# Gate and up of four expert ranks with the weights stationary and the tokens moving, with other slot counts

## The chip, the cores and the metric

One core of a Trainium2 chip runs the kernel; the other cores are idle. The metric is device time in microseconds (us) of one execution, as the median of several; lower is better. The engines are TensorE (PE; its weight loads are listed apart as PEld), VectorE (DVE), ScalarE (ACT), GpSimd (POOL) and SyncE (SP), beside 16 DMA engines.

## The reference

Two layers over 512 latent tokens (and 256 context tokens in the first one), width 1024. Layer 0 is a pooling and attention mixer and a dense SwiGLU, layer 1 latent attention and a mixture of eight experts, of which each token takes two. The change is in the experts:

```python
def moe_swiglu(h, router_w, w_gate, w_up, w_down):
    probs = jax.nn.softmax((tok @ router_w).astype(F32), axis=-1)
    top_p, top_e = lax.top_k(probs, TOP_K)
    top_p = top_p / jnp.sum(top_p, axis=-1, keepdims=True)
    ...
    hg = lax.ragged_dot(xs, w_gate, group_sizes)
    hu = lax.ragged_dot(xs, w_up, group_sizes)
    ys = lax.ragged_dot(jax.nn.silu(hg) * hu, w_down, group_sizes)
```

Each expert has gate and up of 1024 x 2816 and down of 2816 x 1024, all in float32. 512 tokens with two experts each make 1024 rows over the eight experts.

## The kernel before

**Split products.** Every float32 operand is split in two fp32r parts: hi is a rounded copy (`nc.scalar.copy`, ScalarE) and lo the rest (VectorE), both by `split` (L133). `mm3` (L108 to L110) makes a product of three matmuls: hi by hi, hi by lo, lo by hi. The first operand of a matmul is stationary (loaded into the array, a PEld record), the second one moves through it, a column at a time.

**Ranks and slots.** The experts are sorted by their number of tokens on the chip, and rank r gets a fixed count of slots, `CAPS[r]` (L32). A rank's slots are cut in tiles of up to 128 tokens (`rank_tiles`): 256 slots are two tiles, 192 one of 128 and one of 64. Tokens beyond a rank's slots would go to overflow tiles, run by a loop at the end (up to `NOVF` of them, each reading one expert's weights again); the loop runs as often as the routing finds such tiles. Results are written to the DRAM tensor `y_d`, from which each token gathers its two rows. Rows that no expert writes in time are zeroed first (L1220, at the start of `out_and_route`, six writes of 128 x 1024 on the POOL queue).

**One expert** (`expert`, L1503) works in 11 blocks of 256 hidden columns. For a block, `unit` (L1467) loads three pieces of 1 MB of weights (u_raw) and splits each into u_hi and u_lo: two for gate and up, one for down.

- `gate_up(b)`: for each tile of tokens, the tokens x (8 groups of 128 rows of the model width) are stationary, and the weights move: 512 columns, 256 of gate and 256 of up. The sum stands in one PSUM bank (tile name pz, two banks). A tile of 64 tokens (`half`) has its hi and lo side by side as one stationary of 128 columns (L1489, with one more matmul of 64, L1490), two matmuls in place of three; `fold` (L1494) then adds the two halves of the sum. ACT makes silu of the gate half (L1522), DVE the product with the up half (L1523), into sg, tokens by hidden columns.
- `turn(b)`: PE transposes sg in two pieces (L1531) into a bank named ptr or prb, and `split` makes hs of it, hidden columns by tokens.
- `down(b)`: hs is stationary, the down weights move, 512 columns at a time; sums stay in PSUM (pS), or are added up in SBUF (yacc) for the ranks of the second track while the first one runs.

The program gives gate and up of block b+1 ahead of down of block b, and turn of b+1 after it. Two tracks run interleaved: ranks 2, 0, 1 on one, ranks 3, 5, 6, 7, 4 on the other. `flow` (L55) lays their steps on one line: rank 2 beside the end of 3 and beside 5, rank 0 beside 6, rank 1 beside 7, rank 4 last with the rest of the line to itself. The framework that builds the program sets the final order on each engine and all waits.

**Token tiles.** `turn_tile` (L1439) transposes gathered tokens on PE and writes x, hi and lo, with the norm's gain and shift; `RUN_UP` says how many steps ahead of an expert each tile is gathered and turned.

**Names.** x: tokens; u_raw, u_hi, u_lo: weights; sg: gated hidden values; hs: their split transposes; pz, ptr, prb, pS: PSUM banks. L292, L408, L818 and L973 are lines of layers 0 and 1 ahead of the experts.

Of the kernel before, what the change touches and what calls it, by code (L numbers as in the profile page):

```python
# [18 lines left out]
D = 1024  # L19
KT = 8  # L20
# [10 lines left out]

CAPS = (256, 256, 192, 128, 128, 128, 64, 64)  # L32
NSLOT = sum(CAPS)
NOVF = 5
TRACKS = ((2, 0, 1), (3, 5, 6, 7, 4))
# [27 lines left out]
class Kernel:  # L63
# [484 lines left out]
    def layer0_mixer(self):  # L548
        nc, I, tc = self.nc, self.I, self.tc
        self.mix_d = self.dram.tile([KT - 2, 128, TA], F32, name="mix_d")  # L550
        with ExitStack() as ctx:
# [31 lines left out]
            blat = scaled(0, LAT)  # L583
            self.cos = self.const.tile([128, TL], F32, name="cos")
            self.sin = self.const.tile([128, TL], F32, name="sin")
            self.rot = self.const.tile([128, 128], F32, name="rot")
            self.pw = wk.tile([128, 2, 128], F32, name="poolw")
# [428 lines left out]
    def layer1_mixer(self, ctx):  # L1016
# [179 lines left out]
    def out_and_route(self, ctx):  # L1196
# [9 lines left out]
        nc.gpsimd.dma_start(rw, I["router"])  # L1206
        rc = wk.tile([128, 80], F32, name="rc")
        nc.gpsimd.dma_start(rc, I["rconst"])
        iota8, c7, lt = rc[:, 0:8], rc[:, 8:16], rc[:, 16:80].rearrange("p (a b) -> p a b", b=8)
        cb = wk.tile([128, 256], BF16, name="cb")  # L1210
        cf = wk.tile([128, 256], F32, name="cf")
# [127 lines left out]

        nc.vector.tensor_scalar(cap, rank, 5.5, None, op0=OP.is_lt)  # L1340
        nc.vector.scalar_tensor_tensor(cap, rank, 2.5, cap, op0=OP.is_lt, op1=OP.add)
        nc.vector.scalar_tensor_tensor(cap, rank, 1.5, cap, op0=OP.is_lt, op1=OP.add)
        nc.vector.tensor_scalar(cap, cap, 64.0, 64.0, op0=OP.mult, op1=OP.add)
        nc.vector.scalar_tensor_tensor(base, rank, 6.0, rank, op0=OP.min, op1=OP.add)
        nc.vector.scalar_tensor_tensor(base, rank, 3.0, base, op0=OP.min, op1=OP.add)
        nc.vector.scalar_tensor_tensor(base, rank, 2.0, base, op0=OP.min, op1=OP.add)
        nc.vector.tensor_scalar(base, base, 64.0, None, op0=OP.mult)
        nc.vector.tensor_sub(o, n, cap)
# [89 lines left out]

    def turn_tile(self, xg):  # L1439

        n = xg.shape[0]
        X = self.parts(self.xq, "x", 8, KT, n)
# [7 lines left out]
    def parts(self, pool, tag, bufs, k, n):  # L1450

        x = [pool.tile([128, k, 128], F32R, name=tag, bufs=bufs) for _ in range(n // 64)]
        return x if n == 128 else [x[0][:, :, :64], x[0][:, :, 64:], x[0]]

# [39 lines left out]
    def fold(self, ps):  # L1494

        nc = self.nc
        n = ps.shape[1]
        lo = self.xp.tile([64, 512], F32, name="fold", bufs=1)[:, :n]
        nc.scalar.copy(lo, ps[64:])
        nc.vector.tensor_add(lo, ps[:64], lo)  # L1500
        return lo

    def expert(self, reg, X, store, acc=None):  # L1503

        nc, xp = self.nc, self.xp
        NB = F // 256
        T = len(X)
        half = [len(x) == 3 for x in X]
        Y = acc or [self.ps.tile([128, D], F32, name="pS", bufs=2) for i in range(T)]
        H = {}  # L1510

        def gate_up(b):
            U = [self.unit(reg, 3 * b + i) for i in range(2)]
            U = [[v.rearrange("p (k f) -> p k f", f=512) for v in u] for u in U]
            for i in range(T):
# [4 lines left out]
                n = p.shape[0]  # L1520
                sg = xp.tile([128, 256], F32, name="sg", bufs=4)[:n]
                nc.scalar.activation(sg, p[:, :256], AF.Silu)  # L1522
                self.gated = nc.vector.tensor_mul(sg, sg, p[:, 256:])  # L1523
                H[b, i] = sg

        def turn(b):
            for i in range(T):
                n = H[b, i].shape[0]
                pt = self.tr_tile()[:, :2, :n]
                for k in range(2):  # L1530
                    nc.tensor.transpose(pt[:, k, :], H[b, i][:, k * 128:k * 128 + 128], self.ident[:n, :n])  # L1531
                h = self.parts(xp, "hs", 9, 2, n)
                self.split(h[0], h[1], pt)
                H[b, i] = h

        def down(b):
            dh, dl = self.unit(reg, 3 * b + 2)
            for i in range(T):
                h = H.pop((b, i))
                for s in range(2):  # L1540
                    o = s * 512
                    w = lambda k: (dh[:, k * D + o:k * D + o + 512], dl[:, k * D + o:k * D + o + 512])
                    y = Y[i][:, o:o + 512]
# [3 lines left out]
                    p = self.tr_tile().rearrange("p a b -> p (a b)")  # L1547
                    self.mm_tile(p, h, w, 2)
# [4 lines left out]

        gate_up(0)
        yield
        turn(0)
        for b in range(NB):
            if b + 1 < NB:
                gate_up(b + 1)
            down(b)  # L1560
            if b + 1 < NB:
                turn(b + 1)
                yield
        for i in range(T):
            n = 64 if half[i] else 128
            y = (acc[i] if acc else xp.tile([128, D], F32, name="xg", bufs=3))[:n]
            for s in (slice(0, 512), slice(512, 1024)):
                nc.vector.tensor_mul(y[:, s], self.fold(Y[i][:, s]) if half[i] else Y[i][:, s],
                                     self.g2row[:n, s])
            store(i, y)  # L1570
# [24 lines left out]

    def gather_y(self, acc, j, pool, place, tag, bufs):
# [4 lines left out]
        ys = [place.tile([128, D], F32, name=tag, bufs=bufs) for _ in range(2)]  # L1601
        for c, y in enumerate(ys):
# [14 lines left out]
    def moe(self, ctx):  # L1617
# [3 lines left out]
        with ExitStack() as c:  # L1621
            self.moe_pools(c, 2)
            xp = self.xp
            X, G, Sw, todo = {}, {}, [], {}
            order = flow()
# [10 lines left out]

            def turn(t, first):
                if first:
                    G[t] = self.turn_tile(G[t])
                X[t] = next(G[t], X.get(t))  # L1640
# [12 lines left out]
            def weigh():  # L1653

                with behind(tc, self.gathered):
                    nc.gpsimd.dma_start(fg, self.I["final_g"].to_broadcast([128, D]))
                sw = self.xq.tile([128, 2, 512], F32R, name="x", bufs=8)
                Sw.extend((sw[:, 0, :], sw[:, 1, :]))
                OH = self.onehot(last[0], self.i128)
# [13 lines left out]
            def sums(j):  # L1673

                with behind(tc, self.gated):
                    if j > 1:
                        next(G[j - 2], None)
                    if j < 4:
                        G[j] = self.gather_y(A[j], j, xp, *((self.xq, "x", 8) if j % 2 else (xp, "xg", 3)))
                        next(G[j])  # L1680
# [15 lines left out]
            def merge(y):  # L1696

                yh, yl = (self.xq.tile([128, D], F32R, name="x", bufs=8) for _ in range(2))
                for s in (slice(0, 512), slice(512, 1024)):
# [8 lines left out]

            x = X[rank_tiles(FIRST)[0]] = self.parts(self.xq, "x", 8, KT, 128)
            self.x_ins = [self.affine_half(x, 4 * i, pt, (nc.scalar, nc.vector)[i]) for i, pt in enumerate(self.first)]  # L1710
            E = {}
            for p, (r, step) in enumerate(order):
                if step == 0:
# [7 lines left out]
                    acc = [xp.tile([128, D], F32, name="yacc", bufs=1)] if p < at(TRACKS[0][-1], STEPS - 1) and r in TRACKS[1] else None  # L1721
                    E[r] = self.expert(reg, [X[t] for t in rank_tiles(r)], store, acc)
                next(E[r], None)
# [32 lines left out]
    def run(self):  # L1756
        with ExitStack() as ctx:
# [4 lines left out]
            with ExitStack() as c:  # L1762
                self.nraw, self.nhl = 3, 4
                self.wp = self.pool(c, "wp")
                self.big = self.pool(c, "big")
# [72 lines left out]
def layouts(inp):  # L1838
# [38 lines left out]
    e = np.arange(8, dtype=np.float32)  # L1877
    rc = np.concatenate([e, 7 - e, (e[None, :] < e[:, None]).astype(np.float32).reshape(-1)])
    A["rconst"] = np.ascontiguousarray(np.broadcast_to(rc, (128, 80)))
    p = np.arange(128, dtype=np.float32)  # L1880
# [39 lines left out]
```

## Time and profile before

| what | us |
|---|---|
| median of 3 runs (2325.4 to 2331.2) | 2327.38 |
| the profiled execution | 2319.6 |
| its span, first to last instruction | 2317.9 |
| PE busy in the span | 2251.2 |
| VectorE busy | 1765.4 |
| ScalarE busy | 1212.2 |
| GpSimd busy | 198.3 |

The granted clock of TensorE was 0.989 of full speed as a mean of the span. The experts take the time from about 1308 us to the end. In the rows further down, times are microseconds from the start of the span. Records of matmuls and of weight loads are longer than the distance between two of them, because they are pipelined: their pace is the distance between starts. A shape such as 128\*128 128x512 is the stationary (rows by columns) and then the output (rows by moving columns). "x8" is a count of like instructions merged in one line, and "<-DVE u_lo" behind an idle time names what ended it.

### The profile page before, as it was taken

The page shows a single profiled execution, that of the slowest core. Times are in us where ns is not written, and L with a number is a line of the kernel's source. Part 1 is how long each engine was busy: PE and PEld are TensorE (multiplying, and loading weights), DVE is VectorE, ACT ScalarE, POOL GpSimd, SP SyncE. Part 2 cuts the span into 40 slices and gives each one's busy share as a digit, 9 for nine tenths or more (in the row PEclk, how much of TensorE's full clock was granted, in tenths as well). Part 3 has the DMA queues.
Part 4 walks back from the last instruction along what each step waited for, and adds up shares of the span by engine and source line. Part 5 has one row for each costly group of instructions (what it writes and reads, how often), then busy time and mean ns, then how long its engine had stood idle before and what let it go on. Part 6 is the DMA issues. An engine that isn't in the chain of part 4 may idle for free.

```text
span 2317.9 us, 31085 instructions
## 1 busy us (share of the span) xinstructions
PE 2251.2 (97%) x11672; PEld 1833.2 (79%) x11672; DVE 1765.4 (76%) x2547; ACT 1212.2 (52%) x1690; POOL 198.3 (9%) x273
## 2 busy tenths in 40 slices
PE   8999998999999999999999899999999999999996
PEld 3777777899999988888888777777777777777774
DVE  4779876687877876477775798787877778777897
ACT  3445553453334432245553676566655666555764
POOL 0033410000000111000000000010000000000030
PEclk9999998999999999999999999999999999999998
DMA  7233322335444596311122797787777877777794
GB/s 295 80 105 106 107 77 95 110 132 165 143 141 152 198 377 240 126 42 42 35 85 78 275 362 293 282 304 274 266 276 275 315 263 288 267 285 272 275 399 175
DMA packets 97505, 467.97 MB, mean 202 GB/s; under 512 B 11232, under 2 KB 13664, under 8 KB 63556
## 3 DMA queue, kind: packets, MB, share of 16 engines
q1 hardware_dynamic: 76000, 386.83, 45.9%
q0 software_dynamic: 19680, 76.90, 9.2%
q10 hardware_dynamic: 1668, 2.18, 0.3%
q8 instruction: 94, 1.54, 0.3%
q14 instruction: 63, 0.52, 0.1%
HBM read 435.19 MB, written 30.68 MB: 201 GB/s over the span
## 4 chain that ended last, share of the span: by engine, by line
PE 85%; DVE 6%; ACT 2%; DMA 1%; issue 1%; POOL 0%; DVEq 0%; ACTq 0%
PE pz L109 11%; PE pz L108 11%; PE pz L110 11%; PE pS L818 10%; PE pS L973 5%; PE pz L818 4%; PE pS L108 4%; PE pS L109 4%; PE pS L110 3%; PE pz L1490 3%; PE pz L1489 3%; PE pz L973 2%; PE prb L108 1%; PE prb L109 1%; PE prb L110 1%; DVE u_lo L133 1%
## 5 line engine op out<-in xcount | busy, mean ns | idle before, releaser
L133 DVE TENSOR_TENSOR u_lo<-u_raw,u_hi 128x2048 fp32r<-128x2048 f32 x264 | 601.8, 2285 | 154.7 <-ACT u_hi L133 154.5
L133 ACT CAST u_hi<-u_raw 128x2048 fp32r<-128x2048 f32 x264 | 502.4, 1909 | 199.5 <-issue 69.6
L109 PE MATMUL pz<-u_lo,x 128*128 128x512 f32 x704 | 283.7, 403 | 6.2 <-DVE u_lo L133 6.0
L108 PE MATMUL pz<-u_hi,x 128*128 128x512 f32 x704 | 282.0, 401 | 0.5 <-ACT u_hi L133 0.5
L110 PE MATMUL pz<-u_hi,x 128*128 128x512 f32 x704 | 279.9, 398 | 0.0
L108 PE MATMUL pz<-ah,w_hi 128*128 128x512 f32 (+1 forms) x513 | 183.4, 358 | 1.1 <-DVE n_tmp L325 0.6
L109 PE MATMUL pz<-al,w_hi 128*128 128x512 f32 (+1 forms) x513 | 178.8, 349 | 0.0
L110 PE MATMUL pz<-ah,w_lo 128*128 128x512 f32 (+1 forms) x513 | 178.2, 348 | 0.0
L109 PEld LDWEIGHTS pz<-u_lo,x 128*128 128x128 f32 x704 | 132.5, 188 | 46.0 <-DVE u_lo L133 18.7
L108 PEld LDWEIGHTS pz<-u_hi,x 128*128 128x128 f32 x704 | 132.4, 188 | 29.9 <-ACT u_hi L133 1.0
L110 PEld LDWEIGHTS pz<-u_hi,x 128*128 128x128 f32 x704 | 132.5, 188 | 28.5
L292 DVE SCALAR_TENSOR_TENSOR n_acc<-ms 128x1024 bf16<-128x1024 f32 x80 | 97.4, 1217 | 19.0 <-DMA ms<-in_mod_t_dram 18.9
L108 PEld LDWEIGHTS pz<-ah,w_hi 128*128 128x128 f32 x513 | 97.3, 190 | 14.9 <-issue 0.9
L97 ACT CAST w_hi<-w_raw 128x1024 fp32r<-128x1024 f32 (+2 forms) x69 | 58.6, 851 | 93.3 <-PE pz L109 63.2
L110 PEld LDWEIGHTS pz<-ah,w_lo 128*128 128x128 f32 x513 | 97.2, 190 | 11.0 <-issue 0.5
L109 PEld LDWEIGHTS pz<-al,w_hi 128*128 128x128 f32 x513 | 97.6, 190 | 10.5 <-issue 0.7
L109 PE MATMUL pS<-u_lo,hs 128*128 128x512 f32 x264 | 105.1, 398 | 0.7 <-DVE u_lo L133 0.7
L1489 PE MATMUL pz<-u_hi,x 128*128 128x512 f32 x264 | 105.3, 399 | 0.0
L108 PE MATMUL pS<-u_hi,hs 128*128 128x512 f32 x264 | 104.6, 396 | 0.5 <-ACT hs L133 0.5
L110 PE MATMUL pS<-u_hi,hs 128*128 128x512 f32 x264 | 104.6, 396 | 0.0
L1490 PE MATMUL pz<-u_lo,x 128*64 128x512 f32 x264 | 98.5, 394 | 0.0
L408 ACT ACTIVATE P<-pS,mx 128x768 f32<-128x768 f32 (+1 forms) x104 | 83.3, 804 | 19.7 <-DVE mx L407 19.4
(561 smaller groups left out, 5431.8 us busy)
## 6 DMA issues: line engine op xcount, KB each, us to landing
u_raw<-in_moe_w_dram SPq DMA_DIRECT2D x264, 1024.0 KB, 4.9
ms<-in_mod_t_dram POOLq DMA_DIRECT2D x56, 512.0 KB, 4.9
hr<-hid_d SPq DMA_DIRECT2D x38, 384.0 KB, 6.0
w_raw<-in_w_gate_dram SPq DMA_DIRECT2D x28, 512.0 KB, 3.5
w_raw<-in_w_in_dram SPq DMA_DIRECT2D x27, 512.0 KB, 3.3
u<-in_w_up_dram SPq DMA_DIRECT2D x22, 512.0 KB, 3.7
w_raw<-in_w_dn_dram SPq DMA_DIRECT2D x22, 512.0 KB, 4.7
hid_d<-hm POOLq DMA_DIRECT2D x22, 384.0 KB, 3.1
```

What stands on the lines that cost most here:

```text
L97: nc.scalar.copy(hi[:, :n], raw[:, :n])
L108: nc.tensor.matmul(ps, wh, xh, start=first and i == 0, stop=False)
L109: nc.tensor.matmul(ps, wh, xl, start=False, stop=False)
L110: ins = nc.tensor.matmul(ps, wl, xh, start=False, stop=last and i == n - 1)
L133: return nc.scalar.copy(hi, src), nc.vector.tensor_sub(lo, src, hi)
L292: nc.vector.scalar_tensor_tensor(self.m_junk, w, 1.0, self.crow[:, cd, :], op0=OP.mult, op1=OP.mult, accum_out=self.mods[:, layer, cd, n:n ...
L408: self.exped = nc.scalar.activation(P, S, AF.Exp, bias=nm, accum_out=z)
L818: nc.tensor.matmul(ps, w[m][:, c], x[n][:, k, :], start=first and k == i == 0, stop=k == 3 and i == 2, skip_group_check=True)
L973: nc.tensor.matmul((pl, px)[cd][d], W[w][:, d * 128:d * 128 + 128], x[v][:, s], start=n == i == 0 and not (cd and d % 2), stop=n == NF - 1 ...
L1489: m = [lambda s, e: self.nc.tensor.matmul(ps, x[2][:, k, :], w(k)[0], start=s, stop=e), lambda s, e: self.nc.tensor.matmul(ps[:64], x[0][: ...
L1490: lambda s, e: self.nc.tensor.matmul(ps[:64], x[0][:, k, :], w(k)[1], start=s, stop=e)]
```

## The change

The slots become 216, 216, 192, 128, 128, 72, 64, 64 (1080 in all, before 1216), with up to seven overflow tiles in place of five. For ranks 0, 1, 2 (`APART`) and 5 (`JOINED`) gate and up are done the other way round: pieces of 128 weight columns are stationary and all tokens of the rank (216, 216, 192 or 72) move through them. For rank 5, hi and lo of the tokens lie side by side, so that one matmul of 144 columns makes two of the three products. Gate and up then stand in two banks, hidden columns by tokens, and need no transposing; sg is split as it is. The other ranks are as before. The token tiles get other shapes and buffer counts: per rank one pair of tiles (xa) for the ranks of `APART`, four buffers of x for the rest. `cos`, `sin` and `rot` move to a pool of their own that is closed before the experts, which frees their room. The zeros are written at the start of layer 1's attention, as 32 writes of 128 x 256 in place of six of 128 x 1024. The routing reads each rank's slot count and first slot from a table that comes with `rconst`.

```diff
-CAPS = (256, 256, 192, 128, 128, 128, 64, 64)
+CAPS = (216, 216, 192, 128, 128, 72, 64, 64)
-NOVF = 5
+NOVF = 7
+APART, JOINED = (0, 1, 2), (5,)
...
+        zero = wk.tile([128, 256], F32, name="zero")
+        nc.vector.memset(zero, 0.0)
+        for s in [rank_tiles(LAST)[0][0]] + [NSLOT + 128 * k for k in range(NOVF)]:
+            for q in range(4):
+                nc.gpsimd.dma_start(self.y_d[s:s + 128, q * 256:q * 256 + 256], zero)
...
-        zero = wk.tile([128, D], F32, name="zero")
-        nc.vector.memset(zero, 0.0)
-        for s in [rank_tiles(LAST)[0][0]] + [NSLOT + 128 * k for k in range(NOVF)]:
-            nc.gpsimd.dma_start(self.y_d[s:s + 128, :], zero)
...
+        H = sm.tile([128, 8, 8], F32, name="H")
+        nc.vector.tensor_tensor(H, row(iota8, 8), colb(rank), op=OP.is_equal)
+        for v, table in ((cap, caps), (base, firsts)):
+            nc.vector.tensor_mul(G, H, row(table, 8))
+            nc.vector.reduce_sum(v, G, axis=AX.X)
...
+    def x_tile(self):
+        return self.xq.tile([128, KT * 2 * CAPS[JOINED[0]]], F32R, name="x", bufs=4)
...
+    def moving_parts(self, n, joined):
+
+        if joined:
+            both = self.x_tile()[:, :KT * 2 * n].rearrange("p (k c s) -> p k c s", c=2, s=n)
+            return [both[:, :, 0, :], both[:, :, 1, :], both]
+        return [self.xq.tile([128, KT * CAPS[0]], F32R, name="xa", bufs=4)[:, :KT * n]
+                .rearrange("p (k s) -> p k s", s=n) for _ in range(2)]
...
+        def gate_up_moving(b):
+
+            U, n = units(b), sum(ns)
+            P = [self.ps.tile([128, 512], F32, name="pz", bufs=2) for _ in range(2)]
+            joined = len(XW) == 3
+            m = 2 * n if joined else n
+            mm = lambda o, w, x, s, e: nc.tensor.matmul(o, w, x, start=s, stop=e, skip_group_check=True)
+            for k in range(KT):
+                end = k == KT - 1
+                for j in range(4):
+                    wh, wl = (w[:, k % 4, j * 128:j * 128 + 128] for w in U[k // 4])
+                    p = P[j // 2][:, j % 2 * m:j % 2 * m + m]
+
+                    start = k == 0 and j % 2 == 0
+                    if joined:
+                        mm(p, wh, XW[2][:, k].rearrange("p c s -> p (c s)"), start, False)
+                        mm(p[:, :n], wl, XW[0][:, k, :], False, end)
+                    else:
+                        mm(p, wh, XW[0][:, k, :], start, False)
+                        mm(p, wh, XW[1][:, k, :], False, False)
+                        mm(p, wl, XW[0][:, k, :], False, end)
+            sg = xp.tile([128, 2 * CAPS[0]], F32, name="sgm", bufs=2)[:, :2 * n].rearrange("p (f s) -> p f s", s=n)
+            gate, up = (p[:, :2 * m].rearrange("p (f s) -> p f s", s=m) for p in P)
+            if joined:
+                t = xp.tile([128, 512], F32, name="fold", bufs=1)[:, :4 * n].rearrange("p (x f s) -> p x f s", x=2, s=n)
+                for i, v in enumerate((gate, up)):
+                    nc.scalar.copy(t[:, i], v[:, :, n:])
+                    nc.vector.tensor_add(t[:, i], v[:, :, :n], t[:, i])
+                gate, up = t[:, 0], t[:, 1]
+            nc.scalar.activation(sg, gate, AF.Silu)
+            self.gated = nc.vector.tensor_mul(sg, sg, up)
+            H[b, 0] = sg
...
         def turn(b):
-            for i in range(T):
-                n = H[b, i].shape[0]
-                pt = self.tr_tile()[:, :2, :n]
-                for k in range(2):
-                    nc.tensor.transpose(pt[:, k, :], H[b, i][:, k * 128:k * 128 + 128], self.ident[:n, :n])
-                h = self.parts(xp, "hs", 9, 2, n)
-                self.split(h[0], h[1], pt)
+            o, sg = 0, H[b, 0]
+            for i, n in enumerate(ns):
+                if XW:
+                    src, o = sg[:, :, o:o + n], o + n
+                else:
+                    src = self.tr_tile()[:, :2, :n]
+                    for k in range(2):
+                        nc.tensor.transpose(src[:, k, :], H[b, i][:, k * 128:k * 128 + 128], self.ident[:n, :n])
+                h = self.parts([xp.tile([128, 256], F32R, name="hs", bufs=9) for _ in range(1 + (n > 64))], 2, n)
+                self.split(h[0], h[1], src)
                 H[b, i] = h
...
-        gate_up(0)
+        gate = gate_up_moving if XW else gate_up
+        gate(0)
```

## Rows read from the trace of the kernel before

**Rows 1.** The page: busy time by engine; the chain that ended last, by engine.

```profile
PE 2251.2 (97%) x11672; PEld 1833.2 (79%) x11672; DVE 1765.4 (76%) x2547; ACT 1212.2 (52%) x1690; POOL 198.3 (9%) x273
...
PE 85%; DVE 6%; ACT 2%; DMA 1%; issue 1%; POOL 0%; DVEq 0%; ACTq 0%
```

**Rows 2.** Windows: stretch, us, busy of PE, PEld, DVE, ACT, POOL, PEclk, DMA, GB/s.

```profile
1540.00:1660.00 120.00, 120.00 (x536) 91.46 (x535) 91.81 (x83) 81.50 (x92) 1.08 (x1) 1.00 0.77 282
1660.00:1930.00 270.00, 269.97 (x1207) 204.42 (x1207) 207.11 (x198) 167.40 (x183) 9.11 (x11) 1.00 0.75 280
1930.00:2202.00 272.00, 271.50 (x1190) 206.16 (x1189) 213.74 (x206) 166.71 (x165) 5.44 (x7) 1.00 0.76 278
```

**Rows 3.** Timeline of PE, rank 0's gate: start, us, engine, line, operation, tiles, shapes.

```profile
1713.35 0.39 PE L109 MATMUL pz<-u_lo,x 128*128 128x512 f32 x1
...
1718.46 0.39 PE L110 MATMUL pz<-u_hi,x 128*128 128x512 f32 x1
```

**Rows 4.** Timeline of PE: 384 columns, then 256, first and last of each.

```profile
699.80 0.33 PE L818 MATMUL pS<-T2h,w_lo 128*128 128x384 f32 x1
...
700.84 0.33 PE L818 MATMUL pS<-al,w_hi 128*128 128x384 f32 x1
...
905.53 0.28 PE L973 MATMUL pz<-hl,w_hi 128*128 128x256 f32 x1
...
906.73 0.28 PE L973 MATMUL pz<-hh,w_lo 128*128 128x256 f32 x1
```

**Rows 5.** Groups by form: count, busy us, mean ns, idle before and its releasers.

```profile
L109 PE MATMUL pz<-u_lo,x 128*128 128x512 f32 x704 | 283.7, 403 | 6.2 <-DVE u_lo L133 6.0
...
L109 PEld LDWEIGHTS pz<-u_lo,x 128*128 128x128 f32 x704 | 132.5, 188 | 46.0 <-DVE u_lo L133 18.7
...
L1490 PEld LDWEIGHTS pz<-u_lo,x 128*64 128x64 f32 x264 | 35.5, 135 | 12.3
...
L1424 PEld LDWEIGHTS <-n_tmp 128*128 128x128 bf16 x56 | 1.9, 96 | 1.9 <-issue 1.1 <-DVE yacc L1550 0.3 <-DVE n_tmp L1413 0.3
```

**Rows 6.** Timeline of weight loads (PEld): behind tiny bf16 matmuls, and for 8 columns.

```profile
1517.11 0.27 PEld L1424 LDWEIGHTS <-n_tmp 128*128 128x128 bf16 x8 [0.27 <-DVE hs L133]
...
1517.31 0.19 PEld L110 LDWEIGHTS pz<-u_hi,x 128*128 128x128 f32 x1
...
1517.42 0.19 PEld L108 LDWEIGHTS pz<-u_hi,x 128*128 128x128 f32 x1
...
1267.73 0.86 PEld L1240 LDWEIGHTS pS<-rwa,hm 128*128 128x128 f32 x7
```

**Rows 7.** Timeline of PE about two pairs of transposes, of 128 and of 64 tokens.

```profile
1410.45 0.40 PE L110 MATMUL pz<-u_hi,x 128*128 128x512 f32 x1
1410.68 0.38 PE L1531 MATMUL prb<-ident,sg 128*128 128x128 f32 x2
...
1411.13 0.39 PE L109 MATMUL pz<-u_lo,x 128*128 128x512 f32 x1
...
1411.59 0.40 PE L1489 MATMUL pz<-u_hi,x 128*128 128x512 f32 x1
...
1412.47 0.39 PE L1489 MATMUL pz<-u_hi,x 128*128 128x512 f32 x1
```

**Rows 8.** Timeline of PE, ACT and DVE: end of rank 6's gate, its fold.

```profile
1704.24 0.39 PE L1489 MATMUL pz<-u_hi,x 128*128 128x512 f32 x1
...
1708.70 0.39 PE L1489 MATMUL ptr<-u_hi,hs 128*128 128x512 f32 x1
...
1704.73 0.58 ACT L1499 COPY fold<-pz 64x512 f32<-64x512 f32 x1 [0.16 <-PE pz L1489]
...
1707.90 0.67 DVE L1500 TENSOR_TENSOR fold<-pz,fold 64x512 f32<-64x512 f32 x1
```

**Rows 9.** Timeline of POOL in the routing: its first issue, and the zeros.

```profile
1260.46 0.54 POOL L1206 DMA_DIRECT2D rw<-in_router_dram  x1 [59.73 <-ACT ah L133]
...
1262.87 3.26 POOL L1220 DMA_DIRECT2D y_d<-zero  x6
```

More of the change, by code (lines that the diff above doesn't have):

```diff
@@ L1448, in turn_tile, with parts, token_parts @@
             yield X
-    def parts(self, pool, tag, bufs, k, n):
-        x = [pool.tile([128, k, 128], F32R, name=tag, bufs=bufs) for _ in range(n // 64)]
-        return x if n == 128 else [x[0][:, :, :64], x[0][:, :, 64:], x[0]]
+    def parts(self, tiles, k, n):
+        x = [t[:, :k * 128].rearrange("p (k s) -> p k s", s=128) for t in tiles]
+        return [x[0][:, :, :64], x[0][:, :, 64:], x[0]] if n == 64 else [v[:, :, :n] for v in x]
+    def x_tile(self):
+        return self.xq.tile([128, KT * 2 * CAPS[JOINED[0]]], F32R, name="x", bufs=4)
+    def token_parts(self, n):
+        return self.parts([self.x_tile() for _ in range(1 + (n > 64))], KT, n)
+    def moving_parts(self, n, joined):
[4 more added lines that the diff above has]
+                .rearrange("p (k s) -> p k s", s=n) for _ in range(2)]
     def affine_half(self, X, k0, pt, eng):
@@ L1497, in fold @@
         n = ps.shape[1]
-        lo = self.xp.tile([64, 512], F32, name="fold", bufs=1)[:, :n]
+        lo = self.xp.tile([128, 512], F32, name="fold", bufs=1)[:64, :n]
         nc.scalar.copy(lo, ps[64:])
@@ L1501, in fold, with expert, units @@
         return lo
-    def expert(self, reg, X, store, acc=None):
+    def expert(self, reg, X, store, acc=None, XW=None, ns=None):
         nc, xp = self.nc, self.xp
         NB = F // 256
-        T = len(X)
-        half = [len(x) == 3 for x in X]
+        ns = ns or [128]
+        T = len(ns)
+        half = [n == 64 for n in ns]
         Y = acc or [self.ps.tile([128, D], F32, name="pS", bufs=2) for i in range(T)]
         H = {}
+        def units(b):
+            U = [self.unit(reg, 3 * b + i) for i in range(2)]
+            return [[v.rearrange("p (k f) -> p k f", f=512) for v in u] for u in U]
         def gate_up(b):
-            U = [self.unit(reg, 3 * b + i) for i in range(2)]
-            U = [[v.rearrange("p (k f) -> p k f", f=512) for v in u] for u in U]
+            U = units(b)
             for i in range(T):
@@ L1520, in gate_up @@
                 n = p.shape[0]
-                sg = xp.tile([128, 256], F32, name="sg", bufs=4)[:n]
+                sg = xp.tile([128, 256], F32, name="sg", bufs=2)[:n]
                 nc.scalar.activation(sg, p[:, :256], AF.Silu)
@@ L1539, in down @@
                 h = H.pop((b, i))
+                r = 128 if half[i] else ns[i]
                 for s in range(2):
@@ L1558, in expert @@
             if b + 1 < NB:
-                gate_up(b + 1)
+                gate(b + 1)
             down(b)
@@ L1563, in expert @@
                 yield
-        for i in range(T):
-            n = 64 if half[i] else 128
+        for i, n in enumerate(ns):
             y = (acc[i] if acc else xp.tile([128, D], F32, name="xg", bufs=3))[:n]
             for s in (slice(0, 512), slice(512, 1024)):
-                nc.vector.tensor_mul(y[:, s], self.fold(Y[i][:, s]) if half[i] else Y[i][:, s],
+                nc.vector.tensor_mul(y[:, s], self.fold(Y[i][:, s]) if half[i] else Y[i][:n, s],
                                      self.g2row[:n, s])
@@ L1600, in gather_y @@
         nc.vector.tensor_copy(ix, self.slots[:, j::4])
-        ys = [place.tile([128, D], F32, name=tag, bufs=bufs) for _ in range(2)]
+        ys = [place.tile([128, size], F32, name=tag, bufs=bufs)[:, :D] for _ in range(2)]
         for c, y in enumerate(ys):
@@ L1637, in turn @@
             def turn(t, first):
+                r = next(r for r in range(len(CAPS)) if t in rank_tiles(r))
                 if first:
-                    G[t] = self.turn_tile(G[t])
+                    if r in APART + JOINED:
+                        s0, n = sum(CAPS[:r]), CAPS[r]
+                        if r not in XW:
+                            XW[r] = self.moving_parts(n, r in JOINED)
+                        G[t] = self.turn_tile(G[t], [x[:, :, t[0] - s0:t[0] - s0 + t[1]] for x in XW[r][:2]])
+                    else:
+                        G[t] = self.turn_tile(G[t])
                 X[t] = next(G[t], X.get(t))
@@ L1656, in weigh @@
                     nc.gpsimd.dma_start(fg, self.I["final_g"].to_broadcast([128, D]))
-                sw = self.xq.tile([128, 2, 512], F32R, name="x", bufs=8)
-                Sw.extend((sw[:, 0, :], sw[:, 1, :]))
+                sw = self.x_tile()
+                Sw.extend((sw[:, :512], sw[:, 512:1024]))
                 OH = self.onehot(last[0], self.i128)
@@ L1696, in merge @@
             def merge(y):
-                yh, yl = (self.xq.tile([128, D], F32R, name="x", bufs=8) for _ in range(2))
+                yh, yl = (self.x_tile()[:, :D] for _ in range(2))
                 for s in (slice(0, 512), slice(512, 1024)):
@@ L1721, in moe @@
                     acc = [xp.tile([128, D], F32, name="yacc", bufs=1)] if p < at(TRACKS[0][-1], STEPS - 1) and r in TRACKS[1] else None
-                    E[r] = self.expert(reg, [X[t] for t in rank_tiles(r)], store, acc)
+                    E[r] = self.expert(reg, [X.get(t) for t in rank_tiles(r)], store, acc, XW.get(r),
+                                       [t[1] for t in rank_tiles(r)])
                 next(E[r], None)
```

39 lines of the change are left out of this document (17 added, 22 removed).

## The prediction

> **What bounds the kernel now.** Read the page's totals first: TensorE (PE) is busy for 97% of the span, and the chain that ended last runs over PE for 85% [rows 1]. Then the table of stretches over the experts: from 1540 to 2202 us PE is busy for all but about half a microsecond, while in rank 0's stretch VectorE is at 77%, ScalarE at 62% and the DMA engines at 75%; the granted clock is 1.00, the 2.4 GHz level [rows 2]. So in the stages that the change touches every nanosecond put on PE, or taken off it, moves the end, and the other engines and the weight transfers have about a quarter of their time to spare.
>
> A busy PE says nothing of its pace, since a matmul's record is 0.4 us long and overlaps the next ones. The pace is read from the starts. Of one tile's 24 matmuls of gate and up, 23 start from 1713.35 to 1718.46 us: 5.11 / 22 = 0.232 us each, for 512 moving columns [rows 3]. Seven starts with 384 columns take 1.04 / 6 = 0.173 us each, eleven with 256 columns 1.20 / 10 = 0.120 us each [rows 4]. From 384 to 256 that is 0.414 ns a column plus 14 ns a matmul.
>
> Each matmul also has a weight load of its own, beside the matmul before it. L108 and L109 take the same stationary, yet L109 has 704 loads for 704 matmuls [rows 5]: a repeated stationary is loaded again. The record of a load of 64 columns is 135 ns, of 128 columns 188 ns [rows 5], so the part that grows is 53 ns for 64 columns, about 106 ns for 128. Two places show a load with nothing long beside it. At 1517 us come eight tiny matmuls whose bf16 loads follow each other at (0.27 - 0.10) / 7 = 0.025 us; the fp32r load behind them starts at 1517.31, and the next only at 1517.42, 0.11 us later [rows 6]. And seven loads ahead of matmuls with 8 moving columns span 0.86 us: (0.86 - 0.19) / 6 = 0.112 us each [rows 6]. The matmul there has nothing to stream; the load sets the pace. With 512 columns this was never seen, because 0.11 lies under 0.232.
>
> **The change, part by part.** An expert has 11 blocks of 256 hidden columns.
>
> *Gate and up, before.* A tile of 128 tokens takes 8 x 3 matmuls, one of 64 takes 8 x 2, all of 512 columns. Ranks 0 and 1: 48 each; rank 2: 24 + 16 = 40; rank 5: 24. Together 160 a block, 160 x 0.232 = 37.1 us.
>
> *Gate and up, after.* Now the weights are loaded and the tokens stream: 8 x 4 x 3 = 96 matmuls for each of ranks 0, 1 and 2 with 216, 216 and 192 columns; for rank 5, with both halves joined, 8 x 4 x 2 = 64, half with 144 and half with 72 columns. Together 352 a block. No row has an fp32r matmul of under 256 columns. If columns set the pace, the line through 384 and 256 gives 0.103, 0.094, 0.074 and 0.044 us. But the load of 128 weight columns is there each time, and 0.108 to 0.112 us is longer than all four. I take 0.112, the pace of the stream that loads bound: 352 x 0.112 = 39.4 us. The bounds are 0.108 (the growing part of a load, 106 ns, and 2 ns to hand over) and 0.120 (the 256-column pace, if the 14 ns stand on top of the load too).
>
> The Trainium skill speaks against this change in "TensorE: Matmul & The Clock Gate", section LDWEIGHTS (loading the stationary operand): a load takes the number of its columns over 1.2 per ns, whatever the rows. By that, 128 columns are 106.7 ns, which agrees with the 106 ns worked out above [rows 5]; the sum by it alone would be 352 x 0.1067 = 37.6 us a block.
>
> *Transposes.* The four ranks no longer turn the gated tile on PE, since it comes out turned. A pair of full transposes stretches three starts from 1410.45 to 1411.13, 0.68 us where two steps of 0.232 would be 0.46: 0.22 us. A pair of the 64-token tile: 1411.59 to 1412.47, 0.88 - 0.46 = 0.42 us [rows 7]. Six full pairs (ranks 0 and 1 two, ranks 2 and 5 one) and one half pair: 6 x 0.22 + 0.42 = 1.7 us a block.
>
> *Sum on PE.* Before: 37.1 + 1.7 = 38.8 us a block, 427 us in 11. After at 0.112: 3872 x 0.112 = 434 us. So +6.6 us; at 0.108 -8.9, at 0.120 +37.5; the two are even at 427 / 3872 = 0.1103 us. By rank, with 0.112: ranks 0 and 1 gain 0.8 us a block each, rank 2 loses 0.8, rank 5 loses 1.4. Down keeps its matmuls: 88 or 72 tokens as stationary stream the same 512 columns.
>
> *A new wait for the two pz banks.* One tile used one bank, so a gate could start on one while the other was being read out. The new gate needs both from its first k. Rank 6's matmuls into its bank end at 1704.63, its fold is copied at 1704.73, but the addition on VectorE, queued behind two weight splits, ends at 1708.57: 3.9 us [rows 8]. Behind a waiting matmul stand rank 0's or 1's whole gate and whoever needs its result. In strict order, cover is rank 6's transposes (0.42), its down (8 x 0.232 = 1.86) and the first six matmuls (0.67): 2.95, so 0.95 us short, in about 22 steps 21 us. Rank 5 reads two banks with four operations; with one more addition of 0.67 [rows 8] that is 4.6 us against down's 12 x 0.232 + 0.67 = 3.45: 1.15 x 11 = 13 us. So 0 to 34 us. Near zero is likelier: rank 6's own down starts only at 1708.70 [rows 8], 4 us after its gate, and PE is full all that time [rows 2], so other work is put in its gaps, and the 48 matmuls of the free bank can come first. I take 6.
>
> *What is hidden.* The second weight unit of a gate is due later and the first one freed earlier. What PE ever idled for u_lo at this line is 6.0 us [rows 5], some of it outside these ranks: a gain of 0 to 6, taken as 0. One silu and one product of 432 columns replace two of 256; rank 5 gets two copies and two additions more; all of it is on engines with a quarter to spare. The six zero writes of 0.54 us each on the POOL queue [rows 9] become 32 quarter-width ones, about 17 us of that queue, moved ahead of layer 1's reads of h; POOL idled 59.7 us before its first issue of routing [rows 9], and nobody reads the zeros until the end. If that cover were gone, the h reads would be late by 17 us at most; I cost it at nothing. The slot tables replace eight small operations by five. By the reference's inputs the experts get 215, 215, 181, 121, 98, 67, 64 and 63 tokens, so no overflow tile runs under either list of slots.
>
> Total: 6.6 + 6 = +12.6 us on the profiled execution's 2319.6, 2332; that one lies 7.8 under the median of 2327.4, so 2340 for the median.
>
> **Rivals.** (a) *Columns set the pace* and loads stay hidden, as they are at 512 columns. Per block 192 x 0.103 + 96 x 0.094 + 32 x (0.074 + 0.044) = 32.6 us, 358 in 11, so -69 us, with waits of 6 some 2265. For it: the line from 256 to 384 columns, drawn on to 512, gives 0.226 where 0.232 is seen [rows 3, 4], so down to 256 nothing but columns shows. Against it: [rows 6]. It decides as soon as a load of 128 columns takes under 0.094 us. The Trainium skill's same page, section Back-to-back issue gap, gives an isolated matmul its columns over 2.4 per ns and 2.5 ns; the 0.120 here is 11 ns over that. By it the estimate for 216 columns is 92.5 ns and this rival the result. (b) *A wash:* pace of 0.108 to 0.111, waits near 0: 2318 to 2332. Nothing in the rows excludes it; break-even is 2 ns away. (c) *Load plus hand-over:* 0.120, or the bank waits in full: 2327.4 + 37.5 to + 45, 2365 to 2372, slower by far. For it: 0.120 is the pace of the nearest stream in columns and type. Against it: the 8-column stream has only 4 to 6 ns on top. (d) The change runs overflow tiles after all: each would add a whole expert's weights, 33 pieces of 1 MB, some 120 us at 280 GB/s [rows 2]; against it the counts above.
>
> **How the numbers follow.** Forecast (pace near 0.112, some waits, 2332 to 2365): 0.53. (a) 0.13, (b) 0.17, (c) 0.16, (d) 0.01. A measurement of this kernel can tell about 0.3%, 7 us, from no change. Slower by more: forecast and (c), less the forecast's lower edge, 0.66; faster: (a) and a little of (b), 0.15; within: 0.19. The range leaves out (a), (d) and the far end of (c), together under 0.2: from 2316 (0.108, with a little of the 6 us gained) to 2374.
>
> **What would show it.** Right: in the new gate's stretch, starts 0.11 to 0.113 us apart alike for 216, 192, 144 and 72 columns, weight loads starting back to back, rank 2's and 5's stretch (up to about 1660 us) longer and those of ranks 0 and 1 shorter. Wrong: starts at 0.10 us with 216 and 0.045 with 72 columns, which is (a). The wait term shows as PE idle ahead of a pz matmul, released by VectorE; the transposes of L1531 should fall by 14 x 11. The weakest step is the pace, since no row has this form.

## The result: 2417.8 us, 3.95% slower

After the change the median of four runs is 2417.77 us (2415.55 to 2427.09), beside 2326.73 for the kernel before: a ratio of 1.0395 [1.0365, 1.0426], 91 us more. The sign was forecast; the size was not, since 12.6 were worked out and the range ended at 2374. The profiled execution took 2417.34 us, with a span of 2415.7 and a granted clock of 0.971 of full speed as a mean (0.989 before).

First the page of the kernel after: busy time by engine, the granted clock in 40 slices, the chain that ended last.

```profile
PE 2293.0 (95%) x13630; PEld 1956.9 (81%) x13630; DVE 1754.5 (73%) x2522; ACT 1200.2 (50%) x1668; POOL 204.3 (8%) x299
...
PEclk9999999999999999999999999899999899999999
...
PE 22%; DVE 6%; ACT 4%; issue 2%; DMA 1%; ACTq 0%; DVEq 0%; SPq 0%
```

The count of matmuls answers to [rows 1]: 13630 - 11672 = 1958, which is 192 x 11 more for gate and up less 14 x 11 transposes, so the change runs exactly the instructions that were counted and no overflow tile. PE's share fell from 97 to 95%, though it has more to do. Two of the clock's slices inside the experts fall to 8, where before only the last slice did. The chain no longer holds on to PE (22% where it was 85%), and since its shares add up to a third of the span, it is not used further.

Where in the experts? The table of stretches; columns as in [rows 2]. First a row of the kernel before, then the kernel after.

```profile
1400.00:2200.00 800.00, 799.47 (x3561) 607.80 (x3560) 622.79 (x590) 500.08 (x527) 21.02 (x21) 1.00 0.76 280
```

```profile
1400.00:2200.00 800.00, 751.81 (x4985) 654.88 (x4983) 543.21 (x500) 435.61 (x451) 13.65 (x19) 0.96 0.69 251
...
1500.00:1600.00 100.00, 94.90 (x692) 86.12 (x692) 63.26 (x65) 48.38 (x47) 2.88 (x3) 0.93 0.67 237
1600.00:1700.00 100.00, 100.00 (x762) 90.71 (x760) 69.35 (x65) 61.06 (x78) 0.00 (x0) 1.00 0.70 251
...
1800.00:1900.00 100.00, 88.66 (x558) 75.59 (x557) 65.73 (x60) 50.52 (x44) 4.14 (x6) 0.93 0.73 269
```

Before, PE had almost no gaps here and the clock stood at 1.00: in these 800 us it idled for 0.5 us. Now it idles for 48.2 us, and the granted clock is 0.96. The row of 1600 to 1700 is the one to keep in mind: full of the new matmuls, it has neither a gap nor a drop of the clock. In the other two rows PE has gaps, and the clock is down too.

The gaps have names. The waits of PE in the experts (1400 to 2300 us): waiting engine and tile, what released it, total us, times, longest. First the kernel after, its four longest and one further down, then the longest of the kernel before.

```profile
PE pz L1554 <- DVE fold L1517: 17.8, 15, 3.5
PE ptr L1589 <- DVE sg L1545: 8.0, 7, 1.4
PE prb L1589 <- DVE sg L1545: 7.9, 7, 1.3
PE prb L1427 <- DVE n_tmp L1416: 4.9, 2, 3.4
...
PE pz L1554 <- DVE fold L1575: 1.8, 2, 0.9
```

```profile
PE pz L109 <- DVE u_lo L133: 2.6, 4, 1.1
```

The first is the new gate (L1554), which waits for a pz bank that the fold of rank 6 or 7 (L1517, L1500 in [rows 8]) still reads. The next two are transposes of rank 6's or 7's gated tile (L1589, which was L1531). The fourth is the product of the one-hot marks of a later tile with the token list (L1427, which was L1424). The last is rank 5's gate, which waits for its own banks. Before, no wait in the same stretch came to more than 2.6 us in total.

One step of rank 0 or 1 beside rank 6 shows both. The timeline of PE, then of VectorE, kernel after: start, us, engine, line, operation, tiles, shapes, and in brackets the idle time before it and what ended it.

```profile
1803.19 0.39 PE L1506 MATMUL pz<-u_hi,x 128*128 128x512 f32 x1
...
1805.28 0.38 PE L1554 MATMUL pz<-xa,u_hi 128*128 128x216 f32 x2
...
1805.83 0.28 PE L1554 MATMUL pz<-xa,u_lo 128*128 128x216 f32 x1
1807.04 0.48 PE L1554 MATMUL pz<-xa,u_hi 128*128 128x216 f32 x2 [0.94 <-DVE fold L1517]
...
1807.47 0.27 PE L1554 MATMUL pz<-xa,u_hi 128*128 128x216 f32 x1
1808.81 0.30 PE L1589 MATMUL prb<-ident,sg 64*128 64x64 f32 x2 [1.07 <-DVE sg L1545]
```

```profile
1801.90 4.49 DVE L136 TENSOR_TENSOR u_lo<-u_raw,u_hi 128x2048 fp32r<-128x2048 f32 x2 [2.80 <-ACT u_hi L136]
1806.31 0.68 DVE L1517 TENSOR_TENSOR fold<-pz,fold 64x512 f32<-64x512 f32 x1
...
1808.25 0.42 DVE L1545 TENSOR_TENSOR sg<-sg,fold 64x256 f32<-64x256 f32 x1
```

Rank 6's gate is over at 1803.58. Its addition is behind two weight splits and is done at 1806.99, its product at 1808.67. On PE the down of rank 6 lasts until 1805.28; then come six matmuls of the new gate, into the free bank; then PE stands. From 1805.83 the next start was due 0.11 us later and came after 1.21: 1.10 us lost. Three matmuls further on it is 1.23, for the transposes. Together 2.3 us in this step; the list above has 15 such waits for the bank and 14 for the transposes.

### The profile page after: what moved, and what is told of

It reads as the page before. It is cut to its first block, busy times and chain, and to the rows that moved or that the text cites. A ratio compares the mean times of both kernels' runs of the same rounds, so it can differ in the third digit from the quotient of the medians.

```text
span 2415.7 us, 34958 instructions
## 1 busy us (share of the span) xinstructions
PE 2293.0 (95%) x13630; PEld 1956.9 (81%) x13630; DVE 1754.5 (73%) x2522; ACT 1200.2 (50%) x1668; POOL 204.3 (8%) x299
## 5 line engine op out<-in xcount | busy, mean ns | idle before, releaser
L1554 PE MATMUL pz<-xa,u_hi 128*128 128x216 f32 (+1 forms) x2112 | 389.8, 288 | 19.7 <-DVE fold L1517 17.8
L1554 PEld LDWEIGHTS pz<-xa,u_hi 128*128 128x128 f32 x2112 | 346.5, 204 | 26.8 <-DVE fold L1517 20.5
L1554 PE MATMUL pz<-xa,u_lo 128*128 128x216 f32 (+1 forms) x1056 | 303.5, 288 | 0.0
L1554 PEld LDWEIGHTS pz<-xa,u_lo 128*128 128x128 f32 x1056 | 215.8, 204 | 0.9 <-DVE u_lo L136 0.4
L112 PE MATMUL pz<-al,w_hi 128*128 128x512 f32 (+1 forms) x513 | 178.8, 349 | 0.0
L112 PEld LDWEIGHTS pz<-al,w_hi 128*128 128x128 f32 x513 | 97.6, 190 | 10.5 <-issue 0.7
L111 PE MATMUL pS<-u_hi,hs 128*128 128x512 f32 (+1 forms) x264 | 105.0, 398 | 0.5 <-ACT hs L136 0.5
L112 PE MATMUL pS<-u_lo,hs 128*128 128x512 f32 (+1 forms) x264 | 104.1, 394 | 0.8 <-DVE u_lo L136 0.8
L113 PE MATMUL pS<-u_hi,hs 128*128 128x512 f32 (+1 forms) x264 | 104.2, 395 | 0.0
L410 DVE TENSOR_REDUCE mx<-pS 128x1 f32<-128x768 f32 (+1 forms) x104 | 84.4, 828 | 10.1 <-PE pS L1146 6.8
L101 DVE TENSOR_TENSOR w_lo<-w_raw,w_hi 128x1024 fp32r<-128x1024 f32 (+2 forms) x69 | 68.5, 994 | 30.2 <-ACT w_hi L100 27.0
L136 ACT CAST w_hi<-w_raw 128x1024 fp32r<-128x1024 f32 x44 | 46.2, 1050 | 81.7 <-PE pS L821 44.8
L1554 PE MATMUL pz<-x,u_hi 128*128 128x144 f32 x352 | 81.9, 318 | 0.0
```

The lines of the kernel that those rows point to most:

```text
L101: nc.vector.tensor_sub(lo[:, :n], raw[:, :n], hi[:, :n])
L111: nc.tensor.matmul(ps, wh, xh, start=first and i == 0, stop=False)
L112: nc.tensor.matmul(ps, wh, xl, start=False, stop=False)
L113: ins = nc.tensor.matmul(ps, wl, xh, start=False, stop=last and i == n - 1)
L136: return nc.scalar.copy(hi, src), nc.vector.tensor_sub(lo, src, hi)
L410: nc.vector.reduce_max(nm, S, axis=AX.X, negate=True)
```

## Experiments

All times are medians, and the ratios go by the kernel before on the same chip (2325.7, 2327.9 and 2327.4 us for the three groups of runs). No run leaves out any part of the computation. Four theories are in the expectations. A stand is a time in which PE has nothing to run and waits. W: PE stands for the banks, and the clock falls behind a stand; later (W2) it stands for the transposes of rank 6 and 7 as well. L: the weight loads alone set the time. R: the slots, tables and zeros around the new gate cost it. H: the new matmuls themselves bring the clock down, stands or not.

**The rest of the change alone (e2), and rank 5 undone (e3).** All four ranks go back to the old gate, or rank 5 alone does; slots, tables and zeros stay.

```diff
-APART, JOINED = (0, 1, 2), (5,)
+APART, JOINED = (), ()          # e2
+APART, JOINED = (0, 1, 2), ()   # e3
```

> No rank has its weights stationary; the new slot counts, the earlier zeros, the moved angles and the tables stay (buffers of x and of sg as before the change). W and L: as before the change, 2322 to 2332, since the tiles of 88 and 72 tokens move the same 512 columns. R: 2390 or more.

> The changed kernel with rank 5 as it was before (72 tokens stationary), ranks 0, 1 and 2 with the weights stationary. By loads alone rank 5 costs 1.4 us a block more than before: L with all loss in proportion to the surplus of loads: about 15 us less, 2403. W: ranks 0 and 1 beside 6 and 7 keep their stands, rank 5's own stands and cold stretches (before 1600 us) go as well: 15 us of pace and 10 to 20 of stands, 2380 to 2395.

e2: 2319.95, 0.9969 [0.9953, 0.9986]. R falls: without the new gates the change is 0.3% faster than before, 2 us under what W and L gave. e3: 2394.43, 1.029 [1.0269, 1.0312], so rank 5's part is worth 23 us of the 91, and three quarters lie with ranks 0, 1 and 2. That is within W's range and 9 us under L's 2403.

**The free bank first (e1; e4 is e1 with rank 5 undone).** The prediction took the bank wait at 6 us, because the 48 matmuls of the free bank could come first. Here they do: all of the gate's half, then all of up.

```diff
-            for k in range(KT):
+            for k, j in [(k, 2 * f + i) for f in range(2) for k in range(KT) for i in range(2)]:
                 end = k == KT - 1
-                for j in range(4):
+                if True:
```

> The changed kernel, but the new gate does all k of the gate half first (48 matmuls into the bank that is free) and then all k of the up half. Theory W (the loss is PE standing for a PSUM bank that VectorE's addition gives back late, with the halved clock that follows each such stand): the addition ends some 4 us after rank 6's gate, 48 matmuls of 0.111 us are 5.3 us, so the two stands of about 1.1 and 1.2 us in nearly every step and most of the 70 us at half clock go; 2325 to 2350. Theory L (the loads of 128 columns themselves cost the 91 us): the same loads, so 2410 to 2420. Theory R (the rest of the change costs it): 2410 to 2420.

> Rank 5 as before the change and the free bank first. By pace at 0.111 us: ranks 0 and 1 gain 0.9 us a block each, rank 2 loses 0.7, together -12 us in 11 blocks against the kernel before. W: 2312 to 2325, at or a little faster than before. L: about 2403 as with the rank alone.

e1: 2410.78, 1.0355 [1.0332, 1.0378]; e4: 2388.61, 1.0249 [1.0216, 1.0282]. W's numbers are missed by far, in both; e1 lies where L and R had it, e4 14 us under L's number. The waits of PE and the same step of e1 say why:

```profile
PE ptr L1589 <- DVE sg L1545: 15.2, 7, 2.5
PE prb L1589 <- DVE sg L1545: 13.9, 7, 2.3
```

```profile
1800.33 0.27 PE L1554 MATMUL pz<-xa,u_hi 128*128 128x216 f32 x1
1802.87 0.30 PE L1589 MATMUL prb<-ident,sg 64*128 64x64 f32 x2 [2.28 <-DVE sg L1545]
```

The bank wait is gone from the list, and the transposes of the same step stand for all of it: from 1800.33, a start due 0.11 us later came after 2.54, so 2.43 us, where the two stands above were 1.10 and 1.23. They need the product of rank 6, which is ready as late as ever, and PE's order puts them behind its down and only ten short matmuls. So the transposes were the second thing in the same place, and to take one of the two away moved the time by 7 us of 91.

**The transposes later (e6), and both (e5; e7 with rank 5 undone; e8 the kernel before with it).** Ranks that still transpose do so at the start of their next step, instead of at the end of this one (in e8 ranks 3 to 7).

```diff
-        turn(0)
+        if XW:
+            turn(0)
         for b in range(NB):
+            if not XW:
+                turn(b)
             if b + 1 < NB:
                 gate(b + 1)
             down(b)
             if b + 1 < NB:
-                turn(b + 1)
+                if XW:
+                    turn(b + 1)
                 yield
```

> The late transposes alone, the two banks filled side by side as in the change. W2: the stand for the bank is left, some 1.1 us in each of 20 steps, which is 20 to 25 us and the half clock that this still brings on; 2350 to 2390, between the changed kernel and the one with both. If only one stand a step is short enough to leave the clock up: 2345 to 2360. L: 2400 or more.

> The free bank first, and the transposes of the ranks that are not turned round (6 and 7 above all) stand in the program behind the other track's gate and down, no longer ahead of them. Theory W2 (what costs is PE standing, for whatever it is next given of rank 6's or 7's chain of copy, addition, silu and product; with the bank wait gone the transposes took its place, 2.4 us a step): both go, and with them the half clock that follows: 2328 to 2350, half-clock time between 1400 and 2300 us under 25 us. Theory H (the half clock comes from the new matmuls themselves, that stream fewer columns a load, and not from the stands): half-clock time stays at 60 us or more; 2370 to 2390. Theory L (loads): 2400 or more.

> Both, and rank 5 as before the change. W2: pace alone is left, ranks 0 and 1 gain 0.9 us a block, rank 2 loses 0.7: 2308 to 2325. H: 2350 to 2375. L: 2385 or more.

> The kernel before the change with late transposes for the ranks of one tile (3 to 7). W2: PE had no such stands there (the last gap is covered by 29 matmuls of 0.232 us), so nothing to win: 2320 to 2332. If the before kernel also lost to them, 2310 or less.

e6: 2382.58, 1.0237 [1.0201, 1.0273]; e5: 2371.12, 1.0188 [1.0148, 1.0228]; e7: 2335.87, 1.0038 [1.0021, 1.0055]; e8: 2328.33, 1.0001 [0.9983, 1.002]. The later turn is worth nothing to the kernel before, 35 us to the change, and 40 us to e1 (2410.78 to 2371.12). L falls: these kernels run all the loads that L counted, and e5, e6 and e7 lie 29, 17 and 49 us under the least that L gave. e6 and e8 are where W2 had them; e5 and e7 are still above, by 21 and 11 us. H's time is met in e5, but not its clock: 34 us at the 1.2 GHz level, where H wanted at least 60 and W2 under 25. The lists of waits of e5 and e7 have a new head, here of e5, with what follows the longest of these stands on its timeline:

```profile
PE prb L1427 <- DVE n_tmp L1416: 7.5, 2, 4.0
PE ptr L1427 <- DVE n_tmp L1416: 6.3, 2, 3.8
```

```profile
1829.21 0.59 PE L1427 MATMUL ptr<-tokid,n_tmp 128*64 128x2 bf16 x8 [3.78 <-DVE n_tmp L1416]
1829.73 0.76 PE L1554 MATMUL pz<-xa,u_hi 128*128 128x216 f32 x2
1830.29 0.41 PE L1554 MATMUL pz<-xa,u_lo 128*128 128x216 f32 x1
1830.50 0.63 PE L1554 MATMUL pz<-xa,u_hi 128*128 128x216 f32 x2
```

A later tile's one-hot marks are made on VectorE in the step in which PE multiplies them, and PE stood 3.78 us for them. Behind that stand the new matmuls start 0.21 us apart instead of 0.11 (the third of these rows to the fourth): the granted clock is at its 1.2 GHz level.

**The marks a step earlier (e10: all four ranks, e5 and this; e9: e7 and this).** VectorE makes the marks one step before PE needs them.

```diff
+                        plan(g - 1, mark, t)
                         plan(g, gather, t)
```

> The same with rank 5 joined, so the whole change with its stands taken away one by one. W2: four such stands (14 us) and most of the 27 us at half clock go: 2340 to 2355, of which pace alone is 7 over the kernel before. Theory H (joined matmuls of rank 5 bring the half clock on by themselves): the stretches near 1460 and 1550 us stay at half clock; 2355 to 2368.

> Free bank first, late transposes, rank 5 as before, and the one-hot marks of a token tile made on VectorE one step before TensorE's small products need them. Theory W2 (PE standing, and the half clock behind it): the stands of 1.5 to 4.2 us ahead of those products (about 10 us in all) go, with the two stretches of half clock behind them (some 6 us): 2315 to 2328. Theory L (loads alone, 0.112 us each): the pace is as it was, 2333 to 2340.

e10: 2349.78, 1.0094 [1.0076, 1.0111]; e9: 2324.42, 0.9993 [0.9983, 1.0003]. Both are within W2's numbers, and e9 is 9 us under L's. e10 runs every matmul of the change (its page counts 13630 too), and the table of stretches for e5, then e10, holds the answer on H:

```profile
1400.00:2200.00 800.00, 776.99 (x5283) 673.66 (x5282) 569.41 (x525) 461.08 (x472) 15.43 (x19) 0.98 0.73 267
...
1500.00:1600.00 100.00, 93.96 (x670) 85.55 (x670) 61.27 (x66) 47.25 (x46) 4.67 (x3) 0.91 0.63 229
```

```profile
1400.00:2200.00 800.00, 784.48 (x5426) 679.57 (x5425) 587.88 (x548) 475.64 (x491) 18.40 (x19) 1.00 0.75 274
...
1500.00:1600.00 100.00, 98.29 (x758) 89.15 (x758) 68.48 (x71) 52.80 (x52) 4.55 (x3) 1.00 0.71 261
```

The waits for the marks are gone (13.8 us in e5; the same products now wait 4.6 us in all for a bank, none over 1.4). The clock of that stretch goes from 0.91 to 1.00, and 758 matmuls fit in where 670 did. H falls: all the new matmuls run in e10, and its experts have 3.4 us at the 1.2 GHz level, up to the tail, where the kernel after has 85. Nor are they needed for a fall: e8 has none of them, and after a stand of 2.42 us its old matmuls of 512 columns start 0.43 us apart for a while, where 0.23 is usual: the 1.2 GHz level. PE in e8:

```profile
2246.84 0.69 PE L1531 MATMUL ptr<-ident,sg 128*128 128x128 f32 x2 [2.42 <-DVE sg L1523]
...
2248.61 0.63 PE L109 MATMUL pz<-u_lo,x 128*128 128x512 f32 x1
2249.04 0.63 PE L110 MATMUL pz<-u_hi,x 128*128 128x512 f32 x1
```

**Ranks 0 and 1 alone (e11), and its control (e12).** By the pace, only these two gain. e11 gives ranks 2 and 5 the old gate and keeps the three remedies; for want of memory it has four buffers for raw weights instead of five (and of the gated tiles and x one fewer each), and e12 is the kernel before with those four.

```diff
-APART, JOINED = (0, 1, 2), (5,)
+APART, JOINED = (0, 1), ()
...
-        i = 1 if len(self.wraw) > 1 and self.nunit % 5 > 2 else 0
-        raw = self.wraw[i].tile([128, 2048], F32, name="u_raw", bufs=3 - i)
+        i = 1 if len(self.wraw) > 1 and self.nunit % 4 > 2 else 0
+        raw = self.wraw[i].tile([128, 2048], F32, name="u_raw", bufs=3 - 2 * i)
```

> Only ranks 0 and 1 with the weights stationary, with all three remedies; to make room one weight buffer less (four raw ones) and seven x buffers. By pace ranks 0 and 1 gain 0.83 us a block each: 18 us off the kernel before, against its own control with four raw buffers. W2: control - 10 to - 18, 2308 to 2320 if the buffer costs nothing. L as first put (any turned rank loses): 2335 or more.

> The control: the kernel before with four raw weight buffers for five. PE was full and the transfers had a quarter to spare, so 2322 to 2335; if the start of the experts, where the transfers are at 0.94, needs the fifth, 5 to 15 us more.

e11: 2323.96, 0.9982 [0.9971, 0.9993]; e12: 2330.16, 1.0016 [1.0005, 1.0027]. e11 is 6 us better than its control where W2 gave 10 to 18: too large. And these 6 us can't be put down to the new gate: e11 has the rest of the change, which alone was worth 6 (e2), and its control has not. It has the lowest ratio of the versions with a new gate, with e9's interval overlapping its own, and is no better than e2, which has none.

## Why the prediction was right in sign and wrong in size

**The pace (352 matmuls a block at 0.112 us): right.** The timeline of PE in the kernel after, 24 starts of rank 0's gate from the first row to the second, then 12 of rank 5's joined gate:

```profile
1809.25 0.27 PE L1554 MATMUL pz<-xa,u_lo 128*128 128x216 f32 x1
...
1811.93 0.27 PE L1554 MATMUL pz<-xa,u_lo 128*128 128x216 f32 x1
```

```profile
1457.09 0.31 PE L1554 MATMUL pz<-x,u_hi 128*128 128x144 f32 x1
1457.24 0.24 PE L1554 MATMUL pz<-x,u_lo 128*128 128x72 f32 x1
...
1458.43 0.31 PE L1554 MATMUL pz<-x,u_hi 128*128 128x144 f32 x1
```

2.68 / 24 = 0.112 us, and 1.34 / 12 = 0.112 us. 216 columns cost as much as 144 and 72 do on average, the load sets the pace, and rival (a) is out. The Trainium skill, "TensorE: Matmul & The Clock Gate", section LDWEIGHTS (loading the stationary operand), gives columns over 1.2 per ns for a load, 106.7 ns here; the trace agrees to about 5 ns. The estimate of 92.5 ns by its section Back-to-back issue gap is not what these rows show.

**The bank wait (0 to 34 us, 6 taken): this step failed.** It took 19.6 us (17.8 for ranks 6 and 7, 1.8 for rank 5). For ranks 6 and 7 the mechanism was put rightly, and so was its upper end: 0.95 us a step worked out, 1.10 seen. Rank 5's 13 us at the upper end hardly came. What failed is the reason for going to the low end, "other work is put in its gaps, and the 48 matmuls of the free bank can come first". They don't: the program's order on PE goes from bank to bank at every k, and in the trace only six of them precede the wait. That PE was full while rank 6's fold was slow [rows 2, 8] showed that the old order covered it, with matmuls of 0.232 us each; the change halves the very matmuls that made the cover.

**The transposes of rank 6 and 7: the second step that failed, since it is not in the sum at all.** They were counted as cover (0.42 us) and are themselves a wait: rank 6's product ends 5.1 us after its gate (1803.58 to 1808.67). Before, other ranks' matmuls of 0.232 us lay between; now a down of eight and ten short ones do. The two rows of waits come to 15.9 us. e1 shows this wait by itself, 29 us in the two rows; e6 takes it away and leaves the banks.

**The clock: not in the sum either.** Counted from the distances between PE's starts in the experts, the kernel after spends about 85 us at the 1.2 GHz level, in 16 falls of 3.4 to 10.2 us each; the kernel before has none until its very end. Each of the 16 has a stand of PE in the 3 us before it. What a fall costs shows in two stretches of rank 0's gate, 88 of its matmuls with a fall and 86 without (table of stretches, kernel after):

```profile
1758.02:1769.56 11.54, 11.54 (x90) 11.54 (x89) 7.17 (x5) 2.64 (x3) 0.00 (x0) 0.85 0.68 267
1784.44:1794.13 9.69, 9.69 (x88) 9.69 (x87) 6.51 (x4) 2.63 (x3) 0.00 (x0) 1.00 0.75 292
```

PE is busy throughout both; the first takes 1.85 us longer, 0.22 of it for its two more matmuls. While the clock is down, matmuls of L1554 start 0.214 us apart instead of 0.112, so that nearly half of the time at that level is lost; for the 85 us, less some 6 in which PE stands, that is about 40. The kernels' time at that level falls with their stands: 85 us after, 78 in e1, 48 in e6, 34 in e5, 3.4 in e10.

**The sum.** The table of stretches from 1308 us to the end, before, after and e10:

```profile
1308.00:2317.90 1009.90, 984.79 (x4385) 750.62 (x4383) 811.12 (x800) 632.47 (x655) 46.47 (x34) 0.99 0.77 288
```

```profile
1308.00:2415.70 1107.70, 1024.87 (x6347) 872.44 (x6347) 803.82 (x781) 623.87 (x635) 38.37 (x34) 0.96 0.71 264
```

```profile
1308.00:2350.20 1042.20, 994.97 (x6392) 842.29 (x6391) 799.32 (x785) 630.49 (x641) 53.48 (x35) 0.99 0.76 283
```

PE stands for 82.8 us where it stood for 25.1, the tail with it: +58; the clock +40; the pace +7; the rest -6 (e2). That makes 99, where the two profiled executions are 98 apart and the medians 91. The same for e10: stands +22, clock +2, pace +7, rest -6, together 25, and 22 measured. For e9 and e11 it gives +3 and -4 where -3 was measured each time (what e11's fewer buffers cost is in its stands). The medians and the profiled executions of these kernels differ by up to 8 us, so a sum of this kind is good to some 10. It also says what the right sign was worth: the pace of +7, which gave it, and the rest of -6 nearly cancel, and what was measured is stands, taken at 6, and the clock, not taken at all.

**Rank by rank.** Rank 5 costs 25 us (e10 less e9) where its pace gives 1.4 x 11 = 15; 5.6 more are stands between 1395 and 1715 us (PE idles there for 6.4 us in e10 and 0.8 in e9), and the rest of that stays open. Ranks 0 and 1 should have gained 0.8 x 22 = 18 us by their pace; e11 brings 6 against its control, which is no more than the rest of the change brings without them. Its stands are 15 us over those of before (39.8 us from 1308 us on, 10 over its control), for u_lo and for banks at the marks' products and the gathered rows above all, and about 10 us run at the lower clock. That these two take the gain is by the counts; no run removes them.

**What was costed at nothing.** For the zeros that was right: 32 writes are issued from 1050 to 1068 us, and the kernel e2, which has them, is not slower. It was right for u_lo too: PE idled for it at L109 for 6.0 us [rows 5], and in the kernel after it idles for 6.0 us at L112, which here is the gate of ranks 3 and 4 alone, so nothing of it was there to gain. No overflow tile ran. That e2 is 0.3% faster than before was not expected and was not looked into; of its parts, none was run alone.

## What to carry to other kernels

When a change makes the matmuls of one stage shorter, count the cover again for every wait that the fixed order hides behind them, in microseconds and not in instructions: the bank, the transposes and the marks had each been covered while the matmuls were long. If a wait vanishes and the time doesn't move, look in the waits for what now stands in the same place, and take all of them away before judging the idea (here 91 us became 22). At the 216 moving columns and fewer of this kernel the weight load sets the pace, so swapping the operands can pay only where matmuls times 0.112 us is the smaller sum, with the waits counted in. Here it paid nowhere: no version with a new gate is faster than e2, which has none.

## What the hardware showed that was not expected

After gaps of 1 to 4 us in a stream that is otherwise full, TensorE's granted clock fell to its 1.2 GHz level 16 times in the kernel after, for 3.4 to 10.2 us each, while a stretch with the same matmuls and no gap kept 1.00. With the 58 us of added stands went 40 us of lost clock. Not every gap did it. The step shown under the result, with stands of 1.10 and 1.23 us, ran at 1.00, and so did e10 from 2255 to 2305 us, with 8 us of gaps among old matmuls. Which gaps bring the clock down stays open. And two matmuls that each have a load share it unevenly: in the joined gate 144 columns hold PE for 0.15 us and 72 for 0.07, which together are two loads of 0.112.
